# Moving the split of u and y between stores and loads in a hybrid attention/S5 block, and loading some operands earlier

## The chip, the cores and the metric

The kernel runs on one core of a Trainium2 chip. The metric is the device time of one execution in microseconds, as the median of several runs. The core's engines are TensorE (PE, with its weight loads shown as PEld), VectorE (DVE), ScalarE (ACT), GpSimd (POOL) and SyncE (SP). SP computes nothing here; it issues DMAs. ACT and POOL issue some DMAs as well, in the same strict order as their other instructions.

## The reference

One layer of a streaming encoder on 1040 positions (16 learned meta tokens and 1024 inputs) of width 1024. After an RMSNorm one projection gives queries, keys and values of 8 heads of 64, a forget logit per head, the S5 input u (512 wide) and two gate vectors of 1024. Two branches read them:

```
y_a = forgetting_attention(q, k, v, f) @ w_attn_out     # logits q.k/8 + F[t] - F[s], F = cumsum(log_sigmoid(f + b))
z   = gelu(s5(u))                                       # x_t = lam*x_{t-1} + B u_t ;  y_t = Re(C x_t) + D u_t
zg  = z @ w_glu;   y_s = zg[:, :1024] * sigmoid(zg[:, 1024:])
h   = h + (sigmoid(g0) * y_a + sigmoid(g1) * y_s) @ w_o
```

Then comes a gated feed-forward with a causal convolution of width 3 over 5632 channels, its residual, and a final RMSNorm; the meta tokens are dropped. The S5 model has 32 groups of 16 channels with 64 complex states each.

## The kernel before

Features of all 1040 positions live in SBUF as a high and a low part (`xhi`, `xlo`), and every product is three matmuls: high by high, high by low, low by high. The code is written in one program order; a scheduler then puts the instructions of each engine, and the DMAs of each issuing queue, in an order by that priority and by when it reckons them ready. Each engine and queue works strictly in the resulting order. Edges without a semaphore (`after`) fix some of it by hand.

**The projection to u** (lines 282 to 394). The first 272 positions come transposed from the host (`x0t`) and need no transposes: eight feature chunks are scaled by the norm's gain (lines 350 and 353) and multiplied with `w_u` into four PSUM banks, one per 128 channels m (`part`, lines 325 to 329). The token tiles `xt` of 128 rows are loaded meanwhile (`load_x`, lines 310 to 314), in the order 1, 2, 3, 4, 5, 6, each behind the one before. `factors` (line 334) squares and sums a tile on ScalarE (`norm_factor`, line 174) and takes the reciprocal root on POOL (line 178). The factors of tiles 0 (the meta tokens), 1 and 2 are needed as a row `rsB` (lines 364 to 372), by which the first four banks are multiplied into `us` (line 377); this frees the banks. `features` (line 338) scales a tile by its factor on VectorE (line 340), transposes it on TensorE (line 191) and writes `xhi` and `xlo` (lines 193 and 194). Tiles 3 and 4 are the next block of 256 positions, and tiles 5 to 8 the two after it; each block is one more pass of `part`, copied to `us` on ScalarE (line 387). The norm's `sq` buffer is a single one.

**u, the S5 part and y** (lines 391 to 420, function `ssm` from line 1415). u is laid out by chunks of 8 positions: `us[m]` holds 128 channels by 8 steps j by 130 chunks n. The S5 part works on partitions (step j, channel c of a group), so u is turned by a trip through DRAM. The stores cut it: eight DMAs per m of 16 partitions each, on SP for even m and on POOL for odd m (line 394), of 65 KB in runs of 520 bytes. A load of `U` is one DMA of whole rows of 4160 bytes per quarter of 8 groups (line 1694). For each quarter `tables` builds the matrices `Gm`, `Tm` and `Wi` (lines 1642 to 1688; `Tm` is filled by eight DMAs on SP, line 1672), and `chain` (lines 1690 to 1745) does the input product (line 1700), the recurrence on VectorE, the output product (lines 1740 and 1742), the gelu on ScalarE (line 1744) and one whole-row store of y on ScalarE's queue (line 1745). Quarters 0 and 1 are begun ahead, and 2 and 3 when one ends (lines 416 to 421).

**Gates beside it.** TensorE's spare time here goes to the gate chunks 8 to 15 (lines 431 to 453), three passes of 24 matmuls each. Their weights are loaded on POOL (line 140), cast to `whi` on ScalarE (line 146), negated into `wlo` (line 135), and completed by a DMA on POOL that adds the weights (line 136). The results go through `gs` on ScalarE (line 443) to `g_d` in DRAM (line 444). The first two projections of queries and keys use the same weight path.

**z and the GLU** (lines 456 to 621). `load_z` (line 536) reads y back into `zt` (positions in the free dimension, channels on partitions) in 32 DMAs of 65 KB on SP (line 543), splits it, and builds sums of it on VectorE and POOL (lines 558 to 561). `forget_w` (line 462) loads the forget weights `fraw` on SP and makes `wf` on POOL (lines 465 to 467); it is called after `load_z` (lines 605 and 606). Its tiles come from a pool that takes the memory which the gates' pool gave back. TensorE then runs the first query and key projection, the forget product (`forget`, lines 518 and 519, with Exp and Ln on ScalarE at lines 524 and 525), and the GLU (`glu`, with `seven`, lines 200 to 240). Attention, output projection and feed-forward follow.

## Time and profile before

| | |
|---|---|
| median of 3 runs | 1503.91 us (1502.39 to 1506.95) |
| profiled execution | 1505.85 us, its span 1503.6 us |
| mean granted TensorE clock | 0.987 |
| PE busy | 1447.3 us (96%) |
| DVE busy | 1058.6 us (70%) |
| POOL busy | 746.8 us (50%) |
| ACT busy | 713.6 us (47%) |

The span is the time from the first to the last instruction of the profiled execution. Busy time is a sum of instructions, so it says little of where an engine waited; the view of waits lists the idle time of an engine and which instruction ended it. Windows are stretches of the span with the busy time of each engine in them, and the chain of waits follows the work that ended last back from releaser to releaser. The granted clock is TensorE's clock as a share of its full 2.4 GHz, averaged over the stretch. All of the code that the change touches runs in the first 300 us of the span.

### The profile page before, as it was taken

The numbers are of one execution on the slowest core, as the hardware profiler recorded it, in microseconds if no ns is written. First come the engines' busy times: TensorE is split into PE (matmuls) and PEld (weight loads), VectorE is DVE, ScalarE is ACT, GpSimd is POOL, SyncE is SP. The second block draws the span as 40 slices with busy tenths as digits, with TensorE's granted clock in tenths as the row PEclk, the third lists the DMA queues.
The fourth block names the chain that finished last, engine by engine and source line by source line (L and its number), as shares of the span: only waits on it lengthen the run. The fifth ranks groups of instructions, "written<-read, shape, count | busy, mean of one in ns | idle before, by whom it ended". The sixth has DMA issues, their size and how long they took to land.

```text
span 1503.6 us, 26570 instructions
## 1 busy us (share of the span) xinstructions
PE 1447.3 (96%) x9712; PEld 1364.3 (91%) x9712; DVE 1058.6 (70%) x2173; ACT 713.6 (47%) x1384; POOL 746.8 (50%) x854
## 2 busy tenths in 40 slices
PE   7999998999999999998999899999999999999997
PEld 7989997998999999998888899999999999778886
DVE  6888747871657676644468957888787775798795
ACT  6335575531646565552645434444444444444343
POOL 1411127760546556524862134555544425699766
PEclk9999999999999999998999999999999999999999
DMA  6366562551127332167884125666654214774413
GB/s 243 89 162 150 132 151 65 163 168 41 34 78 194 103 82 93 43 222 213 258 168 165 57 85 148 188 185 185 175 137 112 78 57 169 299 234 128 137 50 112
DMA packets 92182, 208.80 MB, mean 139 GB/s; under 512 B 14778, under 2 KB 25658, under 8 KB 91668
## 3 DMA queue, kind: packets, MB, share of 16 engines
q1 hardware_dynamic: 69956, 161.83, 32.6%
q0 software_dynamic: 15872, 34.63, 13.0%
q10 hardware_dynamic: 6224, 10.65, 1.9%
q8 instruction: 76, 1.25, 0.3%
q14 instruction: 54, 0.44, 0.1%
HBM read 167.99 MB, written 69.35 MB: 158 GB/s over the span
## 4 chain that ended last, share of the span: by engine, by line
PE 78%; DVE 8%; DMA 6%; POOL 3%; issue 2%; ACT 2%; SPq 0%; POOLq 0%; DVEq 0%; ACTq 0%
PE mm L161 4%; PE mm L159 4%; PE mm L160 4%; PE sp L221 4%; PE sp L219 4%; PE sp L220 4%; PE mm L219 3%; PE tp L219 3%; PE mm L221 3%; PE tp L220 3%; PE tp L221 3%; PE mm L220 3%; PE tp L756 2%; PE po L778 2%; PE po L777 2%
## 5 line engine op out<-in xcount | busy, mean ns | idle before, releaser
L159 PE MATMUL mm<-xhi,whi 128*128 128x342 f32 (+2 forms) x488 | 159.4, 327 | 1.0 <-DVE q L129 1.0
L161 PE MATMUL mm<-xhi,wlo 128*128 128x342 f32 (+2 forms) x488 | 158.3, 325 | 0.0
L160 PE MATMUL mm<-xlo,whi 128*128 128x342 f32 (+2 forms) x488 | 157.7, 324 | 0.0
L1164 POOL TENSOR_TENSOR ov<-ov,og 128x1024 f32<-128x1024 f32 x21 | 50.6, 2412 | 125.4 <-ACT og L1163 121.7
L129 DVE TENSOR_TENSOR sw<-sf,sw 128x512 fp32r<-128x512 f32 x72 | 66.2, 919 | 50.6 <-ACT sw L1059 50.6
L1059 ACT CAST sw<-sf 128x512 fp32r<-128x512 f32 x72 | 44.9, 624 | 109.8 <-POOL sf L1141 75.3
L159 PEld LDWEIGHTS mm<-xhi,whi 128*128 128x128 f32 x488 | 92.0, 188 | 2.1 <-PE sp L714 0.8
L161 PEld LDWEIGHTS mm<-xhi,wlo 128*128 128x128 f32 x488 | 91.8, 188 | 0.3
L160 PEld LDWEIGHTS mm<-xlo,whi 128*128 128x128 f32 x488 | 91.9, 188 | 0.2
L763 ACT CAST th<-tp 128x256 fp32r<-128x256 f32 (+3 forms) x120 | 56.2, 472 | 61.4 <-PE tp L756 29.2
L1141 POOL TENSOR_TENSOR sf<-raw,sf 128x512 f32<-128x512 f32 x36 | 58.7, 1632 | 49.3 <-DVE sw L129 48.3
L1141 POOL TENSOR_TENSOR sf<-raw 128x512 f32<-128x512 f32 x36 | 47.7, 1324 | 71.6 <-ACT sw L1059 28.3
L129 DVE TENSOR_TENSOR tl<-tp,th 128x256 fp32r<-128x256 f32 (+3 forms) x120 | 65.1, 547 | 25.5 <-ACT th L763 24.0
L221 PE MATMUL mm<-xhi,sw 128*128 128x258 f32 (+1 forms) x288 | 81.0, 281 | 0.0
L219 PE MATMUL mm<-xhi,sw 128*128 128x258 f32 (+1 forms) x288 | 80.8, 281 | 0.0
L220 PE MATMUL mm<-xlo,sw 128*128 128x258 f32 (+1 forms) x288 | 80.7, 280 | 0.0
L728 POOL TENSOR_SCALAR pt<-pt,nm 128x144 f32<-128x144 f32 (+4 forms) x72 | 51.9, 733 | 51.5 <-DVE nm L727 50.5
L1226 DVE SCALAR_TENSOR_TENSOR ov<-hv,cwt,ov 128x1024 f32<-128x1024 f32 x36 | 72.4, 2012 | 0.1
L1059 ACT CAST sw<-raw 128x512 fp32r<-128x512 f32 x70 | 43.0, 621 | 51.7 <-PE sp L221 26.6
L726 ACT ACTIVATE pt<-pt,nm 128x144 f32<-128x144 f32 (+4 forms) x72 | 52.9, 735 | 26.7 <-DVE nm L725 26.1
L719 DVE CUSTOM_DVE_ANT_0 pt<-sp,fb 128x328 f32<-128x328 f32 (+8 forms) x112 | 46.4, 430 | 19.6 <-PE sp L714 11.5
L756 PE MATMUL tp<-ident,pt 128*128 128x128 f32 (+1 forms) x360 | 58.2, 270 | 0.1
(707 smaller groups left out, 5707.7 us busy)
## 6 DMA issues: line engine op xcount, KB each, us to landing
raw<-in_w_up_dram SPq DMA_DIRECT2D x44, 512.0 KB, 3.7
t_d<-in_w_dn_dram POOLq DMA_DIRECT2D x44, 256.0 KB, 6.9
ar<-a_d SPq DMA_DIRECT2D x44, 256.0 KB, 5.0
wr<-t_d SPq DMA_DIRECT2D x44, 256.0 KB, 2.9
a_d<-ov SPq DMA_DIRECT2D x21, 512.0 KB, 2.6
wr<-in_w_dn_dram SPq DMA_DIRECT2D x33, 256.0 KB, 3.9
t_d<-in_w_dn_dram SPq DMA_DIRECT2D x22, 256.0 KB, 4.4
t_d<-t_d SPq DMA_DIRECT2D x22, 256.0 KB, 4.8
```

Of the source, the lines that this page charges most:

```text
L129: return eng.tensor_tensor(out_, src, hi.bitcast(F), ALU.subtract)
L159: yield PE.matmul(ps, whi[:, i, :], ahi[:, i], start=(i == 0), stop=False)
L160: yield PE.matmul(ps, whi[:, i, :], alo[:, i], start=False, stop=False)
L161: yield PE.matmul(ps, wlo[:, i, :], ahi[:, i], start=False, stop=(i == k - 1))
L219: PE.matmul(ps, a[0][:, i], bh, start=(i == 0 and not joins), stop=False, skip_group_check=True)
L220: PE.matmul(ps, a[0][:, i], bl, start=False, stop=False, skip_group_check=True)
L221: PE.matmul(ps, a[1][:, i], bh, start=False, stop=(i == kh - 1), skip_group_check=True)
L756: PE.transpose(tp[:kn, o:o + n], p_[:n, k0:k0 + kn], ident[:n, :n])
L763: S.copy(th[:kn, z:tw], tp[:kn, z:tw])
L1059: S.copy(hi, src)
L1141: sums.append(GP.tensor_tensor(f_, a, b, op))
L1226: V.scalar_tensor_tensor(out=o, in0=h_[:, j:SEQ + j], scalar=cwc(j, m), in1=o, op0=ALU.mult, op1=ALU.add)
```

## The change

The DRAM buffers of u and y now have the shape (m, 128 channels, 8 steps, 130 chunks). u is stored by one DMA of whole rows per m, all four on SP, and each load of `U` becomes eight DMAs on SP of 16 partitions each, one per step. y is stored by eight DMAs of 16 partitions each on ScalarE's queue; in the last quarter every other one is on SP. `load_z` reads y in four DMAs of whole rows. `forget_w` is called before `load_z`. At the start the token tiles are loaded in the order 3, 4, 1, 2, 5, 6; the factors of tiles 3 and 4 are taken before those of tiles 0 to 2; and the squares of tiles 0 to 2 are summed on VectorE in one operation instead of on ScalarE.

```diff
-    u_d = dp.tile([SW // P, P, P // GC, NCH], F, name="u_d")
-    y_d = dp.tile([SW // P, P, P // GC, NCH], F, name="y_d")
+    u_d = dp.tile([SW // P, P, CH, NCH], F, name="u_d")
+    y_d = dp.tile([SW // P, P, CH, NCH], F, name="y_d")
...
-    def norm_factor(pl, src, n, bufs=10, sq=None):
+    def norm_factor(pl, src, n, bufs=10, sq=None, vec=False):
...
-        S.activation(sq[:n], src, AF.Square, accum_out=ss[:n])
+        if vec:
+            V.tensor_tensor_reduce(out=sq[:n], in0=src, in1=src, scale=1.0, scalar=0.0, op0=ALU.mult, op1=ALU.add,
+                                   accum_out=ss[:n])
+        else:
+            S.activation(sq[:n], src, AF.Square, accum_out=ss[:n])
...
-    for i in range(1, 7):
+    for i in (3, 4, 1, 2, 5, 6):
         load_x(i)
...
-        return norm_factor(n1, place[i][:n], n)
+        return norm_factor(n1, place[i][:n], n, vec=i < 3)
...
+    ahead = {i: factors(i) for i in (3, 4)}
     rs0 = [factors(i) for i in range(3)]
...
-        ready = features(i, factors(i))
+        ready = features(i, ahead[i])
...
     for m in range(4):
-        um = u_d[m].rearrange("(j c) g n -> g c j n", c=GC)
-        for g in range(P // GC):
-            (GP if m % 2 else SY).dma_start(um[g], us[m][GC * g:GC * g + GC])
+        SY.dma_start(u_d[m], us[m])
...
-            ym = y_d[m].rearrange("(j c) g n -> g c j n", c=GC)
-            for g in range(GQ):
-                SY.dma_start(zt[GC * g:GC * g + GC], ym[g])
+            SY.dma_start(zt, y_d[m])
...
+    forget_w()
     T4 = load_z()
-    forget_w()
...
-            SY.dma_start(U, u_d[qt])
+            uq = u_d[qt].rearrange("(g c) j n -> j c g n", c=GC)
+            for j in range(CH):
+                SY.dma_start(U[GC * j:GC * j + GC], uq[j])
...
-            S.dma_start(y_d[qt], Y)
+            yq = y_d[qt].rearrange("(g c) j n -> j c g n", c=GC)
+            for j in range(CH):
+                (SY if qt == 3 and j % 2 else S).dma_start(yq[j], Y[GC * j:GC * j + GC])
```

## Rows read from the trace of the kernel before

**Rows 1.** Waits of TensorE, 0 to 300 us: total us, times, longest us.

```profile
PE mm L518 <- POOL wf L129: 3.5, 1, 3.5
PE sp L1700 <- ACT Wi L1684: 3.1, 1, 3.1
PE sp L191 <- DVE vr L176: 3.1, 1, 3.1
...
PE sp L191 <- DVE xlo L129: 1.7, 1, 1.7
```

**Rows 2.** Windows: us, busy us (x) per engine, granted clock, DMA share, GB/s.

```profile
22.00:30.00 8.00, 4.95 (x30) 4.39 (x29) 7.41 (x15) 6.81 (x14) 3.13 (x4) 0.79 0.51 203
...
88.00:98.00 10.00, 6.93 (x31) 6.65 (x30) 5.08 (x11) 4.50 (x11) 0.15 (x2) 0.66 0.59 183
224.00:235.00 11.00, 7.50 (x33) 6.36 (x32) 10.85 (x15) 5.52 (x12) 9.37 (x6) 0.69 0.01 2
246.00:256.00 10.00, 6.03 (x44) 5.20 (x43) 7.50 (x12) 5.69 (x13) 7.72 (x6) 1.00 0.20 60
```

**Rows 3.** Timeline of TensorE, 18.8 to 60 us: start, duration, engine, line, operation.

```profile
28.16 1.01 PE L327 MATMUL mm<-xhi,uh 128*128 128x256 f32 x3
```

**Rows 4.** Timelines of ScalarE and VectorE, 16 to 80 us; in brackets idle time and releaser.

```profile
16.30 1.06 ACT L174 ACTIVATE sq<-xt 128x1024 bf16<-128x1024 f32 x1 [0.29 <-DMA xt<-in_x_dram]
...
18.88 1.06 ACT L174 ACTIVATE sq<-xt 128x1024 bf16<-128x1024 f32 x1 [0.15 <-DMA xt<-in_x_dram]
...
20.88 1.28 DVE L340 SCALAR_TENSOR_TENSOR xt<-xt,rs 128x1024 f32<-128x1024 f32 x1 [0.66 <-POOL rs L178]
...
22.82 1.75 DVE L377 TENSOR_TENSOR usb<-mm,rsB 128x272 f32<-128x272 f32 x3 [0.59 <-ACT rsB L372]
```

**Rows 5.** Groups by line and form, line 719: busy us, mean ns, idle before.

```profile
L719 DVE CUSTOM_DVE_ANT_0 pt<-sp,fb 128x456 f32<-128x456 f32 x8 | 5.0, 627 | 1.1 <-PE tp L756 1.1
```

**Rows 6.** The chain of waits, 60 to 100 us: start, us, what.

```profile
78.09 12.76 DMA U<-u_d
...
91.95 1.24 PE sp L1700 x4
...
97.50 0.29 PE po L160
```

**Rows 7.** Timelines of SP and ScalarE around u's stores.

```profile
63.40 14.21 SPq L394 DMA_DIRECT2D u_d<-usb  x16
...
69.31 0.35 ACT L387 COPY usb<-po 128x256 f32<-128x256 f32 x1
```

**Rows 8.** DMA issues, 63 to 92 us: count, KB each, median us to landing.

```profile
u_d<-usb SPq DMA_DIRECT2D x16, 65.0 KB, 8.0
```

**Rows 9.** Timelines of SP and POOL, 185 to 262 us.

```profile
189.17 28.99 SPq L543 DMA_DIRECT2D zt<-y_d  x32
...
207.67 0.52 POOL L465 MEMSET wf<- 128x512 f32 x1 [2.28 <-DMA g_d<-gs]
...
227.36 1.04 POOL L129 TENSOR_TENSOR wf<-fraw,wf 128x64 fp32r<-128x64 f32 x1
```

**Rows 10.** Timelines of ScalarE, POOL and TensorE after quarters 0 and 2.

```profile
127.25 0.33 ACTq L1745 DMA_DIRECT2D y_d<-Y  x1
...
131.18 0.87 POOL L136 DMA_DIRECT2D wlo<-in_w_g_dram  x1 [2.17 <-ACT wlo L135]
...
138.96 0.32 PE L161 MATMUL mm<-xhi,wlo 128*128 128x342 f32 x1
...
191.12 0.85 POOL L136 DMA_DIRECT2D wlo<-in_w_q_dram  x1 [18.10 <-ACT wlo L135]
...
202.08 0.29 PE L161 MATMUL mm<-xhi,wlo 128*128 128x272 f32 x1
```

**Rows 11.** DMA issues, 125 to 142 us, and of the whole span.

```profile
wlo<-in_w_g_dram POOLq DMA_DIRECT2D x2, 512.0 KB, 8.0
...
zt<-y_d SPq DMA_DIRECT2D x32, 65.0 KB, 3.3
```

## The prediction

> **What bounds the kernel now.** I began with the page's engine shares, in the table above: TensorE is nearly always busy, and the change neither adds nor removes work of TensorE. So it can only give back time in which TensorE waits or runs at its lower clock. The view of waits, cut to the first 300 us (all that is touched runs there), says where: besides the first weights, TensorE waits for the forget weights `wf` (3.5 us), for `Wi` at line 1700 (3.1), for the row factor of a token tile (3.1) and for `xlo` (1.7) [rows 1]. The windows then price what lies beyond each wait: around the first three the mean granted clock is 0.79, 0.66 and 0.69, that is 1.2 GHz instead of 2.4 for a part of the stretch, and a fourth stretch, 246 to 256 us, keeps 1.00 but has TensorE busy for only 6.03 of 10 us [rows 2]. A mean of 0.66 over 10 us is 6.8 us at the lower level (0.34 x 10 / 0.5). TensorE came back at 91.95, and the matmul at 97.50 still takes 0.29 us, so it worked some 5.8 us at half speed [rows 6]: the drop cost 2.9 us. The 0.69 over 11 us is 6.8 us at the lower level as well; by likeness I put it at 2.9 too.
>
> **Start: load order, squares on VectorE.** Now tile 3's square is the third on ScalarE, at 18.88 instead of the first's 16.30; its scaling on VectorE follows at 20.88, and tile 4's stands behind four `us` multiplies that begin at 22.82 [rows 4]. TensorE waits 3.1 us for tile 4 and starts the next projection block at 28.16, at low clock [rows 1, 3]; I count that as 28.7 at full speed. With tiles 3 and 4 loaded and squared first, their scalings come at about 18.3 (20.88 - 2.58) and 19.6, and their transposes lie beside the first block's matmuls. Next late are the `us` multiplies, which free the PSUM banks. They need the factors of tiles 1 and 2, whose squares are now two reductions on VectorE. The nearest row is the same operation on 456 columns, 627 ns [rows 5]: scaled to 1024, 1.4 us. A two-operand pass over 1024 columns takes 1.28 [rows 4]. I take 1.3. Two scalings and two reductions from 18.3 on end at 23.5; factor, transposes and copy add 1.7 (estimate: tile 3's square ended near 20, and its factor was there 0.9 later, twice that for two engines more), so the multiplies begin at 25.2 and TensorE goes on at 25.9: **2.8 us** less. Bounds: 4.7 if all is gone (3.1 and half of 3.4 us at the lower level), and a loss of 1 if the reductions, or the hand-over of the one `sq` buffer between two engines, come ahead of both scalings. The reduction for the 16 meta rows lies under the wait for the first weights and costs nothing; without that cover it is 1.3 us of VectorE.
>
> **u: four whole-row stores, eight loads per quarter.** Gone are 16 stores of 65 KB on SP (14.21 us from 63.40 on [rows 7]) and 16 on POOL; new are four of 520 KB and seven more loads per quarter, all on SP. The chain shows the present load of `U` landing 12.76 us after 78.09, at 90.85, and TensorE back at 91.95 [rows 6]. In the new order SP waits for the last store's data, copied on ScalarE at 69.31 [rows 7], and then issues eight pieces for quarter 0 from about 70 on. At the old rate (14.21 / 16 = 0.89 us each) that ends at 77; with the landing that such pieces had in this stretch, 8.0 us at the median [rows 8], they are in at 85. TensorE stops for them at 88.9 (91.95 - 3.1), or 86 if the start gains 2.8. So I take wait and drop, 3.1 + 2.9 = **6.0 us**, which is the upper bound; the lower is 0, if they land as late as now. Quarter 1's eight and the `Tm` transfers queue behind them on SP; VectorE's tables are what quarter 1 needs then. POOL loses its 16 issues, and gate weights behind them can only come sooner: nothing counted. Quarters 2 and 3 issue eight pieces for one, an estimated 4 to 7 us more on SP, under the table work that stands before their first matmul: nothing, but the delay reaches TensorE if that cover is shorter.
>
> **z and the forget weights.** SP issues 32 pieces of y from 189.17 over 28.99 us, and only then the forget weights; `wf` is finished on POOL at 228.4 [rows 9]. Four whole-row loads, and the weights ahead of them, make `wf` ready while TensorE still has projections (to 228.4 - 3.5 = 224.9). That removes 3.5 + 2.9 = **6.4 us**; lower bound -2 (rival 1). The first three z loads no longer wait for other pieces, so the sums on z start earlier, and VectorE's backlog (busy 10.85 of 11 us at 224 to 235 [rows 2]) shrinks before the thin stretch at 246 to 256. The forget gate's Exp and Ln stay in that stretch. Of its 4.0 us I take half, **1.9**; bounds 0 and 3.8.
>
> **y's stores in ScalarE's queue are the cost.** Each quarter's one store becomes eight; the last quarter gives four of them to SP. An issue takes 0.33 us at 127.25, and `wlo` of the next gate weights is cast on ScalarE behind it; the DMA that completes it goes out on POOL at 131.18 [rows 10], lands 8.0 us later at the median [rows 11], at 139.2, and TensorE first reads such a `wlo` at 138.96 [rows 10]: no cover is left. Eight issues take 2.6 us, of which about 0.9 lies beside a running cast: 1.7 us of TensorE, in quarters 0 and 1 alike. In quarter 2 the DMA goes out at 191.12 and is read at 202.08 [rows 10]: about 3 us of cover, nothing lost. In all **-3.4 us**; bounds 0 (the cast placed first) and -20 (rival 3). That y now leaves in runs of 520 bytes instead of 4160 I take at no cost: a 65 KB piece of such runs lands in 3.3 us at the median [rows 11].
>
> The Trainium skill speaks against this last line: "DMA: Bandwidth & Descriptors", section "Bandwidth", gives a 64 KB transfer 0.95 us and calls smaller ones descriptor-dominated; section "Issuing engines are not separate DMA queues" adds that a second issuer does not help. By it eight pieces take 7.6 us (an estimate), the last z is that much later, and the 1.9 goes: a sum of 11.8. The old z loads went out 0.91 us apart, which agrees in size, but each was 3.3 us under way, so they overlapped; no run yet shows y stored in pieces.
>
> **Sum.** 2.8 + 6.0 + 6.4 + 1.9 - 3.4 = 13.7 us. The profiled execution took 1505.85 us (span 1503.6), 1.94 above the median of the three runs, 1503.91. I take the sum, made on that execution, from the median: **1490.2 us**. The 1.7 us for `xlo` [rows 1] I leave: `Gm` still has to wait for the memory of tiles 1 and 2.
>
> **Rivals.** (1) *The forget weights do not come ahead.* Their buffers lie where the gate tiles `gs` lay, and the memset of `wf` at 207.67 waited for a `g_d` store [rows 9]. If their load stands first on SP and waits there as well, all z loads queue behind it until about 208. Then the wait for `wf` goes, but one for z takes its place, which with its drop I put at 8.4 us (the present 6.4 and 2 more, since VectorE is full there). The last two gains become -2, the sum 3.4, the time 1500.5. For it: the shared memory, and SP's strict order. Against: three of the four z loads may be placed ahead by their readiness. (2) *U comes no sooner.* The pieces stand behind the fourth store and share the DMA engines with gate weights; landing at 91 they gain nothing, and with a start of 0 the sum is 6.4 + 1.9 - 3.4 = 4.9: 1499. (3) *Slower, by ScalarE's queue.* SP's 32 pieces went out 0.91 us apart (28.99 / 32), because SP also waited for other transfers between them. At 0.91, eight hold ScalarE for 7.2 us, about 6 more than now: 12 us of TensorE idle in quarters 0 and 1, 2 to 3 in quarter 2, and two or three clock drops of 2.9, in all 20 to 23 against gains of 17.1: 1507 to 1510. It decides from about 0.75 us an issue. Against: the issue on ScalarE now takes 0.33 [rows 10].
>
> **Chances.** Forecast 0.64, rival 1 0.12, rival 2 0.13, rival 3 0.08, the rest unnamed. About 0.3% (4.5 us) is what a measurement here tells from no change. Faster by more: the forecast and over half of rivals 1 and 2, 0.78; same 0.14; slower 0.08. The low end of the range takes every upper bound and no cost on ScalarE, 4.7 + 6.0 + 6.4 + 3.8 + 1.7 = 22.6: 1481.3. The high end takes in rivals 1 and 2: 1502.
>
> **What would show it.** Right: no TensorE wait over 1 us for `wf` or at line 1700, granted clock 1.00 in both stretches, the second projection block from about 26 us. ScalarE's cost would show as gate matmuls waiting for a `wlo` DMA after a quarter's y. Wrong: `U` landing after 86, SP waiting on `g_d` ahead of z, or y issues on ScalarE 0.7 us and more apart.

## The result: no faster, and the profile after

The changed kernel takes 1509.35 us (median of 20 runs, 1506.48 to 1512.81), the kernel before, on the same chip, 1506.89 us (median of 20, 1501.46 to 1511.27). The ratio is 1.0019, with a 95% interval of 1.0010 to 1.0028: about 2.9 us slower. That lies within the 0.3% that the prediction called no change, and it is far from the 13.7 us gain of the forecast. The time is above the range (1481.3 to 1502).

The profiled execution of the changed kernel took 1508.85 us. These are the first lines of its page.

```profile
span 1507.1 us, 26530 instructions
...
PE 1449.8 (96%) x9712; PEld 1365.1 (91%) x9712; DVE 1062.7 (71%) x2179; ACT 709.8 (47%) x1378; POOL 740.0 (49%) x838
```

Nothing shows in the shares. The places show in the waits of TensorE in the first 300 us (total us, times, longest us), to be read beside [rows 1].

```profile
PE tp L375 <- DVE rb L374: 2.8, 2, 1.7
PE mm L159 <- DVE q L129: 2.6, 1, 2.6
PE sp L195 <- DVE xlo L129: 1.9, 1, 1.9
...
PE sp L195 <- DVE xt L344: 1.1, 1, 1.1
...
PE mm L521 <- DVE kl L129: 0.7, 1, 0.7
PE mm L161 <- DMA wlo<-in_w_q_dram: 0.7, 1, 0.7
```

All three waits that the change was to remove are gone: for `wf`, for `Wi` at the input product (now line 1703), and for the factor of a token tile. In their place TensorE waits for the factors of tiles 0 to 2 (`rb`), for VectorE's split of the queries (`q`), and a little for tiles, keys and `wlo`. The windows price what lies around these waits, in the columns of [rows 2].

```profile
22.00:30.00 8.00, 4.01 (x22) 2.69 (x21) 6.77 (x18) 5.80 (x12) 5.60 (x5) 0.78 0.52 206
88.00:98.00 10.00, 10.00 (x73) 9.74 (x73) 7.90 (x21) 4.95 (x12) 0.00 (x0) 1.00 0.45 100
213.00:224.00 11.00, 8.40 (x47) 8.12 (x46) 10.53 (x11) 10.18 (x18) 8.20 (x2) 0.84 0.31 89
224.00:235.00 11.00, 10.28 (x64) 9.35 (x64) 10.81 (x18) 5.87 (x13) 6.62 (x7) 1.00 0.01 2
246.00:256.00 10.00, 7.10 (x41) 6.33 (x41) 7.85 (x13) 5.71 (x13) 7.88 (x6) 0.83 0.23 67
```

88 to 98 us is mended: TensorE is busy for 10.00 us at full clock, where [rows 2] show 6.93 at 0.66. The start is no better (4.01 busy, before 4.95), and 213 to 224 us, where the kernel before had 11.00 busy at 1.00, now has 8.40 at 0.84. The stretch at 224 has its clock back, and the one at 246 has lost some. This is the window of the kernel before at 213 us:

```profile
213.00:224.00 11.00, 11.00 (x71) 11.00 (x70) 8.91 (x11) 10.22 (x16) 4.90 (x2) 1.00 0.50 120
```

**How the stages are read below.** The order of TensorE's work hardly changes, so the same matmul can be found in every trace. The lateness of a kernel at a milestone is the start or the end of that matmul in its trace, less that in the trace of before (minus is earlier). It comes from one execution of each, so it is good for the place of a gain or a loss. The clock of that one execution is in it too: after the same wait of 1.9 us for `xlo` near 71 us, the mean granted clock at 66 to 80 us is 1.00 in `u_alone` and `no_start`, 0.88 in the changed kernel and 0.76 in `u_forget_less`. Below 1.00, TensorE ran at 1.2 GHz for a part of the stretch, and (1 - clock) x 14 us gives what that lost: 1.7 and 3.4 us. Gains in time come from the many timed runs. The table gives the milestones by their time in the kernel before.

| us | milestone | changed kernel | no start | start alone | u alone | y and z, forget weights |
|---|---|---|---|---|---|---|
| 67.72 | u projection ends | +3.25 | +1.33 | +3.89 | -0.13 | -0.25 |
| 98.31 | gate work goes on | -1.54 | -4.57 | +1.60 | -6.03 | -0.20 |
| 120.68 | quarter 0, output product | -2.14 | -5.16 | +1.60 | -6.62 | -0.20 |
| 163.40 | quarter 2, tables | +0.13 | -2.23 | +1.60 | -5.94 | +1.57 |
| 216.48 | query projection ends | +5.23 | -0.77 | +1.60 | -5.94 | +10.53 |
| 228.45 | first forget product | +0.79 | -5.20 | +1.01 | -5.38 | +6.25 |
| 238.88 | forget products end | -1.05 | -4.98 | -0.23 | -6.50 | +3.53 |
| 252.39 | thin stretch of the GLU | -0.36 | -3.96 | +3.01 | -3.39 | +2.54 |
| 324.6 | all that is touched is done | -0.05 | -4.28 | +3.20 | -2.83 | +2.36 |

So the changed kernel loses 3.25 us at the start, wins some 5 at `U`, loses 2 after the first quarter's y and 5 before the query projection, and gets the last back. At 324.6 us it stands where the kernel before stood; the rest of its 3.0 us between the two profiled executions (1508.85 against 1505.85) arises later, in code that the change does not touch. The last section comes back to that.

### The profile page after: what moved, and what is told of

Its sections match the earlier page's. It is cut to its first block, busy times and chain, and to the rows that moved or that the text cites. A ratio compares the mean times of both kernels' runs of the same rounds, so it can differ in the third digit from the quotient of the medians.

```text
span 1507.1 us, 26530 instructions
## 1 busy us (share of the span) xinstructions
PE 1449.8 (96%) x9712; PEld 1365.1 (91%) x9712; DVE 1062.7 (71%) x2179; ACT 709.8 (47%) x1378; POOL 740.0 (49%) x838
## 4 chain that ended last, share of the span: by engine, by line
PE 78%; DVE 9%; DMA 4%; issue 3%; POOL 2%; ACT 2%; ACTq 0%; SPq 0%; POOLq 0%; DVEq 0%
PE mm L161 5%; PE mm L159 5%; PE mm L160 5%; PE sp L223 4%; PE sp L224 4%; PE sp L225 4%; PE tp L223 3%; PE tp L224 3%; PE tp L225 3%; PE mm L225 3%; PE mm L223 3%; PE mm L224 3%; PE tp L757 2%; PE po L779 2%; PE po L778 2%
## 5 line engine op out<-in xcount | busy, mean ns | idle before, releaser
L129 DVE TENSOR_TENSOR tl<-tp,th 128x256 fp32r<-128x256 f32 (+3 forms) x120 | 65.1, 547 | 25.0 <-ACT th L764 23.5
L727 ACT ACTIVATE pt<-pt,nm 128x144 f32<-128x144 f32 (+4 forms) x72 | 52.9, 735 | 26.3 <-DVE nm L726 25.7
L1186 PE MATMUL mm<-xhi,sw 128*128 128x344 f32 (+4 forms) x160 | 51.7, 325 | 9.0 <-DVE og L1192 9.0
L720 DVE CUSTOM_DVE_ANT_0 pt<-sp,fb 128x328 f32<-128x328 f32 (+8 forms) x112 | 46.4, 429 | 19.6 <-PE sp L715 10.7
```

Source lines behind the costliest of these rows:

```text
L129: return eng.tensor_tensor(out_, src, hi.bitcast(F), ALU.subtract)
L727: S.activation(pt[:n, :kc], pt[:n, :kc], AF.Exp, bias=nm[:n, 1:2], scale=0.125, accum_out=nm[:n, 2:3])
```

## The experiments

Sixteen kernels were run besides the changed one, each timed against the kernel before on the same chip (its median there was between 1506.54 and 1508.76 us, so ratios are compared and not times). *Start*, *u*, *y and z* and *forget weights* are the four parts of the change. The time gained or lost is (ratio - 1) x 1506.9 us; the intervals reach 1.4 to 2.3 us to either side. Start, u, and y and z with the forget weights, each measured alone, add up to +1.4 us, against +2.9 for all together.

| run | what it is | ratio (95%) | us |
|---|---|---|---|
| no_start | all but the start | 0.9976 (0.9964 to 0.9987) | -3.6 |
| start_alone | the start alone | 1.0019 (1.0009 to 1.0028) | +2.9 |
| u_alone | u alone | 0.9982 (0.9971 to 0.9993) | -2.7 |
| yz_forget | y and z, forget weights | 1.0008 (0.9996 to 1.0019) | +1.2 |
| start_scalar_squares | the start, squares on ScalarE | 0.9989 (0.9978 to 1.0) | -1.6 |
| y_on_sync | no_start, all y pieces on SP | 0.9995 (0.9982 to 1.0008) | -0.8 |
| less_splits | before, fewer splits of z sums | 1.0 (0.9988 to 1.0012) | 0 |
| u_less_splits | u, fewer splits | 0.999 (0.9978 to 1.0002) | -1.5 |
| u_yz_scalar | u, y and z, all y pieces on ScalarE | 0.9989 (0.9975 to 1.0004) | -1.7 |
| u_forget | u and forget weights | 0.9997 (0.9983 to 1.001) | -0.5 |
| u_forget_less | the same, fewer splits | 1.0 (0.9986 to 1.0013) | 0 |
| u_forget_start | u, forget weights, start with ScalarE | 0.9978 (0.9963 to 0.9992) | -3.3 |
| z_on_gpsimd | no_start, two z loads on POOL | 1.0011 (1.0 to 1.0023) | +1.7 |
| k_split_first | u_forget_start, key split ahead of z's | 0.998 (0.9968 to 0.9992) | -3.0 |
| after_scalar_squares | changed kernel, squares on ScalarE | 0.9982 (0.9971 to 0.9993) | -2.7 |
| mended | the same, two z loads on POOL | 0.9988 (0.9977 to 1.0) | -1.8 |

### The start, with and without it

`no_start` is the changed kernel with the start of the kernel before:

```diff
-    for i in (3, 4, 1, 2, 5, 6):
+    for i in range(1, 7):
         load_x(i)
...
-        return norm_factor(n1, place[i][:n], n, vec=i < 3)
+        return norm_factor(n1, place[i][:n], n)
...
-    ahead = {i: factors(i) for i in (3, 4)}
...
-        ready = features(i, ahead[i])
+        ready = features(i, factors(i))
```

`start_alone` is the kernel before with these lines of the changed one.

> The changed kernel with its start as before (load order 1 to 6, all squares on ScalarE, factors of tiles 3 and 4 taken where they are used). Theory A: the start gives back what the rest gains; it cost 3 to 5 us, so this kernel is 3 to 5 us faster than the changed one, some 1 to 3 us faster than the kernel before, and the first gate matmul is back at about 72.3 us. Rival B: the loss sits in ScalarE's stores of y and in the loads of z; then the time stays 2 to 3 us above the kernel before. Rival C: U in pieces gains nothing; then the time is that of the kernel before, with the wait at the input product back.

> The kernel before with the new start alone. Theory A: 3 to 5 us slower than before; the u projection ends near 71 us instead of 67.7, and VectorE's multiplies that free the first PSUM banks begin near 32 us instead of 22.8. Rivals B and C: within 1 us of the kernel before or faster, since they put the loss elsewhere.

Measured: -3.6 us and +2.9 us. The start, which the prediction put at a gain of 2.8, is a loss of 2.9 alone and of 6.5 (2.9 + 3.6) within the change. The timeline of VectorE in the changed kernel shows the order that came out.

```profile
17.86 1.28 DVE L344 SCALAR_TENSOR_TENSOR xt<-xt,rs 128x1024 f32<-128x1024 f32 x1 [0.67 <-POOL rs L182]
...
19.13 1.20 DVE L175 CUSTOM_DVE_ANT_0 sq<-xm 16x1024 bf16<-16x1024 f32 x1
...
20.78 1.28 DVE L344 SCALAR_TENSOR_TENSOR xt<-xt,rs 128x1024 f32<-128x1024 f32 x1 [0.45 <-POOL rs L182]
...
22.05 1.20 DVE L175 CUSTOM_DVE_ANT_0 sq<-xt 128x1024 bf16<-128x1024 f32 x1
...
24.50 1.20 DVE L175 CUSTOM_DVE_ANT_0 sq<-xt 128x1024 bf16<-128x1024 f32 x1
...
28.28 1.28 DVE L344 SCALAR_TENSOR_TENSOR xt<-xt,rs 128x1024 f32<-128x1024 f32 x1
...
30.03 1.28 DVE L344 SCALAR_TENSOR_TENSOR xt<-xt,rs 128x1024 f32<-128x1024 f32 x1
...
31.98 1.21 DVE L382 TENSOR_TENSOR usb<-mm,rsB 128x272 f32<-128x272 f32 x2
```

Tile 3 is scaled at 17.86, close to the 18.3 foreseen. Then the reduction of the 16 meta rows, which the prediction had put under the wait for the first weights, takes 1.20 us between the two scalings. Tile 4 comes at 20.78 instead of 19.6, the reductions of tiles 1 and 2 at 22.05 and 24.50, and two more scalings stand before the `us` multiplies. These begin at 31.98, against 22.82 in [rows 4]; the row that they need, `rsB`, was copied at 29.68 to 30.07, so the last of the scalings, at 30.03, stood in their way and the one before it did not. The second projection block then starts late, `33.00 0.51 PE L331 MATMUL mm<-xhi,uh 128*128 128x256 f32 x1` against 28.16 in [rows 3].

POOL's roots and ScalarE's next square are held up as well, as their timelines in the changed kernel show.

```profile
17.27 0.55 POOL L182 TENSOR_TENSOR rs<-vr,nhalf 128x1 f32<-128x1 f32 x1 [15.50 <-DVE vr L180]
19.29 1.46 POOL L182 TENSOR_TENSOR rs<-vr,nhalf 128x1 f32<-128x1 f32 x1 [1.46 <-DVE vr L180]
22.20 1.46 POOL L182 TENSOR_TENSOR rs<-vr,nhalf 16x1 f32<-16x1 f32 x1 [1.45 <-DVE vr L180]
...
25.79 1.06 ACT L178 ACTIVATE sq<-xt 128x1024 bf16<-128x1024 f32 x1 [0.39 <-DVE ss L175]
...
29.68 0.39 ACT L377 COPY rsB<-tp 128x272 f32<-128x272 f32 x1
```

A root takes 0.55 us alone and 1.46 beside a reduction; the one at 22.20 ends 0.41 us after the reduction that began at 22.05 (22.05 + 1.20 = 23.25, 22.20 + 1.46 = 23.66). The Trainium skill, "SBUF — State Buffer", section "Who interferes with whom", says that a VectorE instruction with two inputs in SBUF and a GpSimd instruction that reads SBUF contend for one shared pair of ports, which is an exclusive lock. The trace agrees: both roots end about 0.4 us after their reduction, a little less than the 0.55 that one takes alone. ScalarE's square of tile 5 goes out at 25.79, behind the last reduction, with which it shares the one `sq` buffer; tile 4's had begun at 17.19.

### The squares back on ScalarE

`start_scalar_squares` is the kernel before with the new load order and `ahead`, and nothing else; `after_scalar_squares` is the changed kernel with one line changed:

```diff
-        return norm_factor(n1, place[i][:n], n, vec=i < 3)
+        return norm_factor(n1, place[i][:n], n)
```

> The kernel before with the token tiles loaded 3, 4, 1, 2, 5, 6 and the factors of tiles 3 and 4 taken first, but every square on ScalarE. Theory A (the squares on VectorE and the shared square buffer delay the multiplies that free the PSUM banks): those multiplies begin near 25 us instead of 32, the u projection ends at or up to 3 us before 67.7, and the time is 0 to 3 us under the kernel before, that is 3 to 6 under the start alone. Rival D (the load order itself is the loss, since the row of factors of tiles 1 and 2 comes late): the projection still ends after 69 and the time is 2 us or more above the kernel before.

> The changed kernel with every square on ScalarE, nothing else altered (load order, factors of tiles 3 and 4 first, u, y, z and forget weights as in the change). Theory A (in the changed kernel, too, it is the squares on VectorE that cost, 4.5 us of the difference between the two start variants measured alone): 3 to 6 us faster than the changed kernel, that is 1 to 4 us under the kernel before; the u projection ends near 67 us instead of 71. Rival: with U in pieces the start no longer decides, and the time stays within 1 us of the changed kernel, above the kernel before.

Measured: -1.6 us and -2.7 us. In both kernels this one edit is worth much the same: 4.5 us (2.9 + 1.6) in the start alone, 5.6 us (2.9 + 2.7) in the changed kernel. In `after_scalar_squares` the multiplies begin 5.3 us sooner, and the projection ends at +0.09 instead of +3.25. These are the lines of VectorE and POOL there.

```profile
26.64 1.76 DVE L382 TENSOR_TENSOR usb<-mm,rsB 128x272 f32<-128x272 f32 x3
...
21.69 0.55 POOL L182 TENSOR_TENSOR rs<-vr,nhalf 128x1 f32<-128x1 f32 x1 [1.08 <-DVE vr L180]
...
29.09 1.52 POOL L182 TENSOR_TENSOR rs<-vr,nhalf 128x1 f32<-128x1 f32 x1 [1.74 <-DVE vr L180]
```

The root is back at 0.55 us where VectorE has no reduction, and at 1.52 where it falls beside a scaling (28.93 to 30.21), which also has two operands. So the squares on VectorE make the start a loss. Which share the queue, the port and the one buffer have was not tried apart.

### u alone

The kernel before with this part:

```diff
-    u_d = dp.tile([SW // P, P, P // GC, NCH], F, name="u_d")
+    u_d = dp.tile([SW // P, P, CH, NCH], F, name="u_d")
...
-        um = u_d[m].rearrange("(j c) g n -> g c j n", c=GC)
-        for g in range(P // GC):
-            (GP if m % 2 else SY).dma_start(um[g], us[m][GC * g:GC * g + GC])
+        SY.dma_start(u_d[m], us[m])
...
-            SY.dma_start(U, u_d[qt])
+            uq = u_d[qt].rearrange("(g c) j n -> j c g n", c=GC)
+            for j in range(CH):
+                SY.dma_start(U[GC * j:GC * j + GC], uq[j])
```

> The kernel before with u stored by whole rows and loaded in eight pieces per quarter, nothing else. Theory A: 5 to 6.4 us faster than before, no wait over 1 us at the input product, granted clock 1.00 from 88 to 98 us. Rival C: no faster, and the wait at the input product is there still or TensorE stops for something else in the same stretch.

Measured: -2.7 us. At its place the gain is the forecast's: 6.03 us at 98.31, 6.62 at 120.68, still 6.50 at 238.88. Then half of it goes: 3.39 is left at 252.39. These are a window and two waits of TensorE in this kernel, in the columns used above.

```profile
228.00:240.00 12.00, 9.71 (x68) 8.32 (x67) 11.83 (x19) 7.29 (x18) 4.25 (x5) 1.00 0.12 44
```

```profile
PE mm L516 <- POOL wf L129: 4.1, 1, 4.1
PE mm L219 <- DVE kl L129: 2.2, 1, 2.2
```

TensorE arrives 6 us earlier at the forget product, waits 4.1 us for `wf` (3.5 in [rows 1]) and then 2.2 for the split of the keys, while VectorE is busy for 11.83 of 12 us. The longer wait for `wf` costs nothing in the end, since the lead is whole at 238.88; the loss lies behind it, where the GLU begins with the wait for `kl`. The question for the next runs was whether the forget weights or VectorE take the gain.

### Forget weights ahead, and less work for VectorE

`forget_w` is called before `load_z`, with u, and z still in 32 pieces (`u_forget`). `less_splits` is the kernel before without the splits of the sums z1, z2 and z3, whose high parts stand for the low ones; `u_less_splits` and `u_forget_less` add that to u and to `u_forget`.

```diff
+    forget_w()
     T4 = load_z()
-    forget_w()
```

```diff
-    T3, T2, T1 = ([zp.tile([P, 2, TH], R, name=f"z{i}{w}") for w in "hl"] for i in (3, 2, 1))
+    T3, T2, T1 = ([zp.tile([P, 2, TH], R, name=f"z{i}{w}") for w in "h"] * 2 for i in (3, 2, 1))
...
-                split_lo(V, lo, f_[:, q:q + TH], hi)
+                if t_ is T4:
+                    split_lo(V, lo, f_[:, q:q + TH], hi)
```

> The kernel before with six of VectorE's splits left out (z1l, z2l, z3l: the high part stands in for the low part in the GLU's products, with the same matmuls), some 4.2 us less of VectorE between 209 and 236 us. It is the base for the next one. Expected 0 to 3 us under the kernel before: TensorE waits here mostly for the forget weights and the GLU's chain.

> u stored by whole rows and loaded in pieces, and the same six splits left out. Theory A (the U part gives TensorE 6.0 to 6.5 us up to 238 us, and VectorE's backlog then takes back 2.3 to 3.7 of it): with VectorE relieved the gain against the kernel with the splits left out alone is 5 us or more, against 2.7 measured with the splits in. Rival E (what is lost is not VectorE's): the gain stays near 2.7.

> The kernel before with u in the new layout and the forget weights called ahead of z; y and z as before, in 32 pieces, so the scheduler puts the forget weights behind the tenth piece instead of the last. Theory A (VectorE's backlog takes back u's gain): no TensorE wait for the forget weights, but nearly as long a one for VectorE's splits of k in its place; as fast as u alone, within 1.5 us. Rival F (the late forget weights take it back): with them ready TensorE keeps 5 us or more of u's gain up to 300 us, and the time is 5 to 8 us under the kernel before.

> The same with the six splits left out as well (z1l, z2l, z3l; the high part stands in for the low part). If two limits of about the same height, the forget weights and VectorE's splits, hold TensorE at 220 to 240 us, then only this one, with both lowered, shows u's whole gain: 5 to 8 us under the kernel with the splits left out alone. If VectorE alone was the limit, it is as fast as u with the splits left out; if the forget weights alone, as fast as the run with u and the forget weights.

Measured: 0, -1.5, -0.5 and 0 us, with intervals of about 2 us to either side. None of these edits gives back what u loses. The longest wait of TensorE there, one line from each of `u_less_splits`, `u_forget` and `u_forget_less`, is:

```profile
PE mm L516 <- POOL wf L129: 4.8, 1, 4.8
```

```profile
PE mm L516 <- DVE kl L129: 4.2, 1, 4.2
```

```profile
PE mm L516 <- DVE kl L129: 3.5, 1, 3.5
```

With VectorE relieved the wait is for `wf`. With `wf` early (`u_forget`), TensorE is 10.01 us ahead at 228.45, but only 5.74 at 238.88, since it waits for `kl` instead. That looks like two limits of about equal height, one behind the other. Taking both away (`u_forget_less`) left a `kl` wait of 3.5, so the splits taken out were hardly those that stand ahead of the keys. Nor can its trace show u's whole gain: with the clock of 0.76 at 66 to 80 us it is only 3.65 us ahead at 120.68, where `u_alone` has 6.62. So that VectorE's work takes half of u's gain is argued from the waits, and no run gave it back.

### The key split ahead of z's

`u_forget_start` is `u_forget` with the start of `start_scalar_squares`. `k_split_first` adds edges that put the second key split ahead of the last z split and of the second half of z's sums, and calls `load_z` after the first projection (`kl_log` lists the key splits, so `kl_log[1]` is the second):

```diff
-    T4 = load_z()
     qk = qk_tiles(0)
     run(project_qk(0, qk))
+    T4 = load_z()
...
-            split_lo(V, zl, zts[m][:, :, :w_], zh)
+            z_ = split_lo(V, zl, zts[m][:, :, :w_], zh)
+            if m == 3:
+                after(z_, kl_log[1])
...
-            V.tensor_tensor(f1, part(0, 1, k), part(0, 0, k), ALU.subtract)
+            z_ = V.tensor_tensor(f1, part(0, 1, k), part(0, 0, k), ALU.subtract)
+            if k:
+                after(z_, kl_log[1])
```

> u in the new layout, the forget weights ahead, the token tiles in the new order with all squares on ScalarE; y and z as before. The parts that were seen to gain, without those that were seen to lose. Theory A: the sum of u's 2.7, the start's 1.6 and what the forget weights add (0 to 3): 4 to 7 us under the kernel before. Rival: they end at the same later limit (VectorE between 220 and 250 us), then no more than u alone, about 2.7.

> The kernel with u, forget weights and the new load order with squares on ScalarE (y and z as before), and two order edges on VectorE: the splits of the second k block ahead of the last z block's split and of the second set of sums on z. Theory A (what stops TensorE for 3.2 us at 222.8 is the place of the k split behind 5 us of z work): this wait falls under 1.5 us, and TensorE stands 2 to 4 us earlier at 240 us than without the edges; at 325 us 0 to 3 of it is left, since the z work is then later. Rival: VectorE's total is the limit, so TensorE waits as long for z a few us later, and nothing is gained at 300 us.

Measured: -3.3 and -3.0 us. VectorE and TensorE of `u_forget_start` show the wait that the edges were to remove.

```profile
221.19 3.19 DVE L129 TENSOR_TENSOR zlo<-zt,zhi 128x1040 fp32r<-128x1040 f32 x1
...
224.72 1.12 DVE L129 TENSOR_TENSOR kl<-mm,k 64x384 fp32r<-64x384 f32 x2
...
226.00 0.55 PE L517 MATMUL mm<-xhi,wf 128*64 128x384 f32 x1 [3.21 <-DVE kl L129]
```

A z split of 3.19 us stands before the key split. In `k_split_first` that wait is gone and TensorE is 11.80 us ahead at 238.88 (7.53 in `u_forget_start`); but its GLU then starts into a wait of its own, on the timeline of TensorE:

```profile
231.21 0.56 PE L219 MATMUL mm<-zhi,ops 128*128 128x260 f32 x1 [4.13 <-DVE kl L129]
```

At 252.39 the lead is 3.86 us, less than the 5.24 without the edges, and the time is the same. That speaks for the amount of VectorE's work between q and the GLU as the limit. It does not settle it: the GLU waits for the third key split, which the edges left where it was, behind two sums of z (229.94 us, and 229.83 without them), and an order with that one first was not tried.

### y, z and ScalarE's queue

`yz_forget` is y in pieces, z in whole rows and the call of `forget_w`. `y_on_sync` is `no_start` with all pieces of y on SP; `u_yz_scalar` is u, y and z with all of them on ScalarE; the latter leaves `forget_w` at its old place.

```diff
-                (SY if qt == 3 and j % 2 else S).dma_start(yq[j], Y[GC * j:GC * j + GC])
+                SY.dma_start(yq[j], Y[GC * j:GC * j + GC])
```

```diff
-                (SY if qt == 3 and j % 2 else S).dma_start(yq[j], Y[GC * j:GC * j + GC])
+                S.dma_start(yq[j], Y[GC * j:GC * j + GC])
```

> The kernel before with y stored in pieces, z loaded by whole rows and the forget weights called ahead of z; u and the start as before. Theory A: the wait for the forget weights goes (about 5.7 us with its clock drop), but VectorE's split of q, queued behind the work on z that waits for the z loads, costs about 4.3 and y's issues on ScalarE about 1; so within 2 us of the kernel before. Rival B: 3 us slower or more, with TensorE waiting for the low part of the gate weights after each quarter's y.

> The kernel with u, y, z and forget weights as in the change and the start as before, but all of y's pieces issued on SP. Theory A (eight issues on ScalarE hold back the casts of the next gate weights): the waits for the low part of the gate weights after quarters 0 and 1 (1.0 us at 135, with what follows some 2.7 by 163 us) go, and TensorE stands 2 to 2.7 us earlier at 165 us than in the kernel with the same start and y on ScalarE; of that 0 to 2 is left at the end, since VectorE is full from 205 to 250. Rival: the pieces cost the same on SP, as U of quarters 2 and 3 queues among them; then no gain at 165 us.

> The kernel with u, y and z as in the change and the start as before, but the last quarter's four pieces of y on ScalarE too, so that SP does not hold the z loads behind them. Theory A: the z loads go out some us ahead of 199.6, the first sums on z leave VectorE free before the q splits are due, and TensorE's wait for q (1.4 us in the kernel with SP's four pieces, 2.6 in the changed one) goes; 1 to 3 us faster than that kernel. Rival G (the z loads wait for the memory of the gate tiles or for y itself): they go out no sooner than 199, and nothing is gained.

Measured: +1.2, -0.8 and -1.7 us. First the pieces. In the changed kernel eight of them take 4.11 us of ScalarE's queue, 0.51 each, and `wlo` waits behind them:

```profile
125.11 4.11 ACTq L1750 DMA_DIRECT2D y_d<-Y  x8
...
132.59 0.86 POOL L136 DMA_DIRECT2D wlo<-in_w_g_dram  x1 [5.71 <-ACT wlo L135]
```

From 120.68 to 163.40 us the changed kernel loses 2.27 us of lead and `no_start` 2.93, where the prediction had 3.4. `u_alone`, whose y is still one store, loses 0.68 there, so the pieces make up 1.6 to 2.3. That looks like the queue. But with them on SP, out of ScalarE's way, the stretch still costs 2.34 (5.33 - 2.99). Here is the DMA that completes `wlo`, on POOL, and the matmul that reads it, first in `no_start`, then in `y_on_sync`.

```profile
129.93 0.86 POOL L136 DMA_DIRECT2D wlo<-in_w_g_dram  x1 [6.06 <-ACT wlo L135]
...
136.25 0.42 PE L161 MATMUL mm<-xhi,wlo 128*128 128x342 f32 x1 [1.00 <-DMA wlo<-in_w_g_dram]
```

```profile
125.84 0.86 POOL L136 DMA_DIRECT2D wlo<-in_w_g_dram  x1 [2.15 <-ACT wlo L135]
...
135.84 0.42 PE L161 MATMUL mm<-xhi,wlo 128*128 128x342 f32 x1 [1.39 <-DMA wlo<-in_w_g_dram]
```

It goes out 4.1 us sooner (125.84 against 129.93) and is read only 0.4 us sooner: it is 10.0 us under way instead of 6.3. Not all of that is the pieces' doing. It now goes out 2.71 us behind the 512 KB load of the next `raw` weights on the same queue (123.13, and 6.7 us under way), which in `no_start` had landed before. In `u_alone` it goes out 2.71 us behind that load as well, with no pieces of y about, and is 7.8 us under way. That leaves some 2.2 us for the pieces and for the loads of `U` that are now among them; that they hold it up in the DMA engines, whichever queue issues them, is argued and not shown. The Trainium skill says in "DMA: Bandwidth & Descriptors", section "Issuing engines are not separate DMA queues", that DMAs of all issuing engines run on the same 16 DMA engines, and with its words on small transfers in "Bandwidth" that is the rule which the prediction weighed and set aside. The cost up to 163 us agrees with it: 2.34 us with the pieces on SP, 2.93 on ScalarE.

Then z. TensorE's longest wait of the stretch is for the split of the queries (4.4 us in `yz_forget`, 2.6 in the changed kernel), which VectorE does behind work on z. In the changed kernel SP's and VectorE's timelines have:

```profile
198.57 2.00 SPq L1750 DMA_DIRECT2D y_d<-Y  x4
...
203.25 3.16 SPq L544 DMA_DIRECT2D zt<-y_d  x4
...
209.78 0.33 SPq L466 DMA_DIRECT2D fraw<-in_w_f_dram  x1
...
214.43 1.10 DVE L561 TENSOR_TENSOR zf<-zt,zf 128x520 f32<-128x520 f32 x1 [0.39 <-DMA zt<-y_d]
...
215.56 1.12 DVE L129 TENSOR_TENSOR q<-mm,q 64x384 fp32r<-64x384 f32 x2
```

The 32 old loads began at 189.17 [rows 9], quarter by quarter as y came. The four new ones go out from 203.25 on, all behind the last quarter's stores, and take 9.2 us to land (3.3 for an old piece [rows 11]). Then VectorE sums z before it splits q. The split of q begins at 215.56, TensorE stands for it and falls to half clock, which makes the +5.23 at 216.48; `yz_forget` has +10.53 there.

Why the loads for quarters 0 to 2 go out that late shows in the waits of SP's queue, 180 to 225 us: in the changed kernel and in `u_yz_scalar`, where all eight pieces of the last quarter are on ScalarE.

```profile
SPq L544 <- DMA y_d<-Y: 3.0, 3, 2.6
```

```profile
SPq L539 <- DMA y_d<-Y: 9.8, 3, 8.8
```

They stand behind stores of y that they don't read. In the program every DMA of these queues takes one of eight completion semaphores in turn and waits for the one that had it before; eight pieces in a row take all eight. That fits the waits. It can't be SP's own pieces alone, since `u_yz_scalar` has none on SP and its first z load goes out at 198.23 (199.56 in `no_start`); nor the memory of `zt` or y itself, since on POOL's queue two of these loads go out at 192.42 (next section). But the semaphores are read from the program, and no run took them alone away, so that part is argued and not shown.

The forget weights did not come ahead of z either: `fraw` goes out at 209.78, behind all z loads. That is still 8 us sooner than in the kernel before, where it stood behind 32 of them (189.17 + 28.99 = 218.16 [rows 9]). But `wf` is done at 225.88, only 2.5 us sooner than the 228.40 there (227.36 + 1.04 [rows 9]), since its rounding on POOL takes 7.36 us. Read from the programs, whole-row z gives the same order of instructions on all five engines whether `forget_w` is called before or after `load_z`, so in the changed kernel that edit does nothing. With z in pieces (`u_forget_start`) it works: `fraw` goes out at 196.50.

### z's loads past SP's queue

`z_on_gpsimd` is `no_start`, `mended` is `after_scalar_squares`, both with the first two z loads on POOL's queue:

```diff
-            SY.dma_start(zt, y_d[m])
+            (GP if m < 2 else SY).dma_start(zt, y_d[m])
```

> The kernel with u, y, z and forget weights as in the change and the start as before, but the loads of the first two z blocks issued on POOL's queue, ahead of the last quarter's y. Theory H (the whole-row z loads go out only at 199.6 us because each stands on SP behind the last quarter's pieces and waits for a DMA of theirs to land): these two go out before 195 us, VectorE's work on them ends before the q splits are due, and TensorE's waits for q and k (1.4, 1.1 and 1.5 us) fall to under 1.5 us together; some 1 to 3 us faster than that kernel. Rival: they go out early, but VectorE is full anyway, and TensorE gains under 1 us at 300 us.

> The changed kernel with both mends: every square on ScalarE, and the first two z loads on POOL's queue. If the theories A and H both hold, 3 to 6 us under the kernel before; if the z loads do not matter, as fast as the changed kernel with the squares on ScalarE.

Measured: +1.7 and -1.8 us, so 5.3 us worse than `no_start` and 0.9 worse than `after_scalar_squares` (the last within the intervals). The loads do go out early; VectorE and TensorE of `z_on_gpsimd` show what follows.

```profile
192.42 1.16 POOL L539 DMA_DIRECT2D zt<-y_d  x2
...
210.45 2.77 DVE L129 TENSOR_TENSOR zlo<-zt,zhi 128x1040 fp32r<-128x1040 f32 x1 [3.62 <-ACT zhi L544]
...
217.51 0.66 PE L159 MATMUL mm<-xhi,whi 128*128 128x384 f32 x1 [6.02 <-DVE q L129]
```

With z reckoned ready sooner the scheduler puts its split ahead of q's on VectorE, where it even waits 3.62 us for ScalarE, and TensorE's wait for q grows to 6.02 us (1.4 in `no_start`). So the theory that q is late because z's loads queue on SP fell: an early load alone does not help, the order on VectorE decides.

## Why the prediction was wrong

**Start: forecast +2.8 of gain, measured a loss of 2.9.** The failed step is "two scalings and two reductions from 18.3 on end at 23.5", and behind it "factor, transposes and copy add 1.7". The size of a reduction was nearly right (1.20 us and 0.07 to read the sum, against 1.3), and so was the first scaling. Wrong was that four operations follow each other without a gap, and that the meta rows' reduction "costs nothing": it went between the scalings, and VectorE stood 0.45 and 0.43 us for roots on POOL, which took 1.46 us beside a reduction, against 0.55. The four ended at 25.7. Factor, transposes and copy then took 4.4 us, to 30.07: the factor stood behind splits on VectorE, and the copy behind squares on ScalarE that had waited for the `sq` buffer. Then a scaling came ahead of the multiplies, 1.9 us more. They began at 31.98 where 25.2 was worked out (2.2 + 2.7 + 1.9 late). The bound of a 1 us loss named one of these causes, the hand-over of `sq`, but only for the case that it comes ahead of both scalings, which it did not.

**u: forecast 6.0, measured 6.0 to 6.6 where it is made and 2.7 in the time.** The wait at the input product and the clock drop are gone, as forecast. In the changed kernel the first matmul on `U` is `93.55 0.61 PE L1703 MATMUL sp<-U,Wi 128*128 128x130 f32 x4`, with no wait before it. The pieces for quarter 0 were in by 85.8 us, as far as the trace has their landing, against 85 forecast and 90.85 before. What was left out is what is late next: the gain was added to the sum as if nothing were behind it. Half of it goes between 238.88 and 252.39 us, at the GLU's waits behind VectorE. The prediction read VectorE's backlog (10.85 of 11 us busy [rows 2]) and put it down as a gain of its own.

**Forget weights: forecast 6.4; the wait went, the time did not.** "Four whole-row loads, and the weights ahead of them" failed: the weights stayed behind z and came 2.5 us sooner instead of 3.5 or more. From 216.48 to 238.88 us the changed kernel wins 6.28 us, the size of the forecast, but from 163.40 to 216.48 it loses 5.10, most of it at the wait for q (2.6 us) and at half clock behind it. Rival 1 holds in its effect (a wait for z's work takes the place of the one for `wf`), though not by its cause: what z stands behind on SP is y's stores. SP's one wait for the gates ahead of z (4.0 us for `gs`, at a load of GLU weights) ends at 192.84, before the last y is there. And where the weights did come ahead, in `u_forget`, a wait of 4.2 us for `kl` came in their place.

**VectorE's backlog: forecast 1.9, measured nothing.** "The first three z loads no longer wait for other pieces, so the sums on z start earlier" is wrong: in whole rows all four loads went out late, and the sums fell on the split of q. From 238.88 to 252.39 us the changed kernel loses 0.7 us where the backlog was to shrink.

**y's pieces: forecast -3.4, measured about -2.3 to -2.9 up to 163 us, 0.7 of it without the pieces.** The size was near, and the mechanism at most half of it: the issues do hold `wlo` back on ScalarE, but with them gone its transfer takes longer and the cost stays. That the runs of 520 bytes come "at no cost" failed: the last quarter's four pieces on SP land after 4.6 us at the median, where the one store of whole rows took 3.0, and z waits for them. The rule that the prediction set aside here would not have saved it, since by it the sum was still 11.8.

**Rivals and chances.** Rival 2 fell: `U` came in time. Rival 3's price did not occur (0.51 us an issue, below the 0.75 from which it decides). The changed kernel is slower, as in rival 3, but by another way, the start and the split of q, and by less than the 4.5 us that count as a difference, so the outcome is the "same" that had 0.14. The second block from about 26 us, named as a sign of being right, did not come (33.00). Two small slips don't matter here: 3.1 and half of 3.4 are 4.8 and not 4.7, and half of 4.0 is 2.0 and not 1.9. The chances and the whole range stood on gains that were added up although the same engine, VectorE, was to serve all of them: it got the squares, and at 210 to 250 us the same work in a shorter time.

## What to carry to other kernels

A gain that TensorE makes upstream is worth no more than the lead that the next full engine leaves of it: look for the window in which another engine has hardly a gap (VectorE's 11.83 of 12 us here), and count gains only as far as that. Work moved to an engine is to be priced by everything that then queues behind it (here 1.20 us a reduction, 5.6 us in the time), and the scheduler's order has to be read for each edit, since a line moved in the source may move nothing. Of this change u's part is worth keeping (-2.7 us alone), and the squares belong on ScalarE. The load order is not shown to help: it has -1.6 alone, with an interval that reaches 0, and the changed kernel with the squares on ScalarE has -2.7 with it (`after_scalar_squares`) and -3.6 without (`no_start`). These two, `u_forget_start` (-3.3) and `k_split_first` (-3.0) beat the kernel before by about 0.2%, and can't be told from each other.

## What was not expected of the hardware

- A GpSimd operation on 128 x 1 elements takes 0.55 us alone and 1.46 to 1.52 beside a VectorE operation of 1.2 to 1.28 us. The rounding of the forget weights on POOL, 0.24 us in the kernel before, is beside a chain of VectorE's splits `218.04 7.36 POOL L469 TENSOR_SCALAR wf<-fraw 128x64 fp32r<-128x64 f32 x1 [1.32 <-DMA fraw<-in_w_f_dram]`; that the splits hold it is argued by likeness.
- A DMA of 512 KB that adds into SBUF lands after 6.3 us when eight y pieces and a load of 512 KB went out well ahead of it, after 7.8 close behind such a load without pieces, and after 10.0 close behind the load and the pieces; the first and the last end within 0.4 us of each other.
- The same wait of TensorE (1.9 us for `xlo` near 71 us) was followed by a mean granted clock at 66 to 80 us of 1.00 (`u_alone`), 0.88 (`u_less_splits`) and 0.76 (`u_forget_less`), in a part of the program that is the same in the three. Why is open.
- The changed kernel's later 3 us stay open. By lateness it loses 1.5 us between 324.6 us and the last transposes at 1493 us, and the rest behind them. Seven of the other kernels (no_start, start_alone, start_scalar_squares, u_alone, yz_forget, after_scalar_squares, u_forget_start) lose 0 to 2.6 us between the same milestones against that one execution of before, in code that is the same in all of them. The lateness at 324.6 us agrees with the time gained or lost within 0.7 us for no_start, start_alone and u_alone, and misses it by 2 to 3 us for start_scalar_squares (+0.57 against -1.6), u_forget_start (-5.93 against -3.3) and the changed kernel (-0.05 against +2.9), and by about 4 for u_forget (-4.49 against -0.5) and u_yz_scalar (-6.03 against -1.7). One execution of a kernel differs from another by as much (1506.48 to 1512.81 for the changed one), so no cause is read from that.
